# Fetching the context stream's mixing inputs ahead, and keeping its residual in DRAM

## The chip, the cores and the metric

The kernel runs on one core of one Trainium2 chip. The metric is the device time of one execution in microseconds, as the median of several runs. The core's engines are TensorE (PE; its weight loads are listed as PEld), VectorE (DVE), ScalarE (ACT), GpSimd (POOL) and SyncE (SP), which here only issues DMAs. TensorE's clock is granted by a throttle and is shown as a fraction of full speed.

## The reference

One step of a hybrid backbone with two layers, run for two streams that share the weights: 256 context tokens and 1024 latent tokens, all in float32, with 1024 model columns. Each layer computes:

```python
h   = rmsnorm(x, norm1_w) * (1 + sc1) + sh1
p   = h @ w_in                      # columns for three mixers
att = block_attention(q, k, v)      # latent queries see cached context keys and latent keys
lru = gelu(p_gate) * (hf + hb)      # bidirectional recurrence after a width-4 convolution
hy  = hyena_mixer(p_hy)             # width-3 convolution, two gated FFT convolutions
x   = x + g1 * (concat([att, lru, hy]) @ w_out)
h2  = rmsnorm(x, norm2_w) * (1 + sc2) + sh2
x   = x + g2 * ((silu(h2 @ ffn_w1) * (h2 @ ffn_w3)) @ ffn_w2)
```

The outputs are both streams' x after two layers, and the context's keys, values and final recurrence states of each layer.

## The kernel before

Activations lie with model columns on the partitions (eight tiles of 128) and tokens along the row. The latent stream has two blocks of 512 tokens, called l0 and l1; the context stream is one block of 256, called cc (`self.ctxs`, `cs`, and `s` where a function serves both). Float32 matmuls are made of three passes over a rounded high part and a remainder (`mm3`, L153 to L155); `split` makes the two parts, a ScalarE copy (L159) and a subtract (L160) that runs on VectorE unless another engine is named.

A planner puts the instructions of each engine in one order ahead of time, from a simulated timeline and from priorities; context mixing (`ctx_mix`) runs at a raised priority (`tc.high_priority(offset=3000)`) among the matmuls of latent Hyena and latent attention. Nearly all DMAs are issued from SP's queue, in that order. Memory in SBUF is given out in scoped pools: a pool that opens where an older one lay waits until the older one's last use, a store included, is over.

One layer runs so: the norm, w_in (its output goes to DRAM as pT, for both streams), the mixers of both streams (each stores its part of mix_l or mix_c to DRAM), w_out, the upper half of the feed-forward part (ffn_up) and its lower half (ffn_down). Of the context stream:

- `ctx_mix` opens a pool for each mixer in turn: cm (attention, L855 to L947), cl (LRU), ch (Hyena).
- `lru_pass` (from L1000) takes for each of two column tiles a gate weight gw (one buffer; GpSimd memset L1004), an input xp with padding (VectorE memsets L1010 and L1011, load L1012), and later a gate input gl (loaded by L1059); its result is stored at L1068 as mix_c<-xc.
- `conv` in Hyena (L1298 to L1306) takes for each of six tiles an input hxp with two padding columns (memsets L1301 and L1302, load L1303) from one pool tag, and the convolution writes hv (ScalarE, L952) and others. The matrices hw (L1320) and the spectra kt (L1234) are loaded there too.
- `w_out` (L453 to L490) loads the mixers' output for the blocks cc, l0, l1 in pieces of two tiles (tile mst for latent, mrow for context; load L467) and splits them into h (L469). The latent residual is loaded here from DRAM (xq<-xd_l, L473); the context residual stays in SBUF for the whole kernel, in the pool gp. `one` does the matmuls of one output tile, adds to the residual (L480) and stores a latent tile back (L482).
- `ffn_down` makes seven passes of eleven steps; the context takes part in passes 1 and 3. The latent residual is loaded in passes 0 and 1, a tile for each of steps 1 to 8 (x_l<-xd_l, L707); weights come as wst<-in_ffn_w_dram (L689) and are split into whl. At the end of layer 0 it also makes the next layer's norm (`nx`) and stores the latent residual again.
- `front0` loads both streams' x, the context's into gp, and stores the latent residual.

Of the kernel before, what the change touches and what calls it, by code (L numbers as in the profile page):

```python
# [87 lines left out]
class Net:  # L88
# [363 lines left out]

    def w_out(self, l, hp, tp, cp):  # L453
        nc = self.nc
        l0, l1, cc = self.all
        blks = (cc, l0, l1)
        for s, bi, b0, N in blks:
            self.h_new(s, bi, hp)
            mv = s.mix[l].rearrange("(k p) t -> p k t", p=128)
            for k0 in KPIECES:  # L460
                if s.lat and bi == 0 and k0 > 3:
                    st = self.wp.tile([128, 2, N], F32, tag="wst", name="mst", bufs=SBUFS)
                elif s.lat:
                    st = tp.tile([128, 2, N], F32, tag="gl", name="mst", bufs=3)
                else:
                    st = self.rows([128, 2, N])
                nc.sync.dma_start(st, mv[:, k0:k0 + 2, b0:b0 + N])  # L467
                h, k = s.h[bi][k0 // 4], k0 % 4
                self.split(st, h[:, 0, k:k + 2], h[:, 1, k:k + 2])  # L469
            if s.lat:  # L470
                s.x[bi] = [cp.tile([128, 4, 512], F32, tag=f"xq{bi}{j}", name=f"xq{bi}{j}") for j in range(2)]
                for d in range(0, 8, XD):
                    nc.sync.dma_start(s.x[bi][d // 4], s.xd[bi][:, d:d + XD])  # L473

        def one(m, w, s, bi, b0, N):
            ps = self.ps(s, "ops", (128, N))
            for i, k in enumerate(KORDER):
                self.mm3(ps, w[:, 0, k], w[:, 1, k], *self.hk(s, bi, k), i == 0, i == 7)
            xs = self.xs(s, bi, m)
            nc.vector.scalar_tensor_tensor(xs, ps, self.mod(l, s, 2, m), xs, ALU.mult, ALU.add)  # L480
            if s.lat:
                nc.sync.dma_start(s.xd[bi][:, m], xs)  # L482
            self.ss_add(s, tp, s.ss[bi], xs, m)

        for g in GROUPS:
            ws = [self.wtile(self.a["w_out"][l][:, m * 128:(m + 1) * 128].rearrange("(k p) m -> p k m", p=128))
                  for m in g]
            for b in blks:
                for m, w in zip(g, ws):
                    one(m, w, *b)  # L490
                if g[-1] == 7:
                    if b[0].lat:
                        self.norm_q(b[0], l, b[1], tp)
                    else:
                        self.norm(b[0], l, 1, b[1], hp, tp)
# [161 lines left out]
    def ffn_down(self, l, hp, pool, xp, last):  # L657
# [13 lines left out]
        def nx(s, bi):  # L671
            if last:
                self.store_y(s, bi, pool)
                return
            self.norm(s, l + 1, 0, bi, hp, pool)
            if s.lat:
                nc.sync.dma_start(s.xd[bi], s.x[bi])

        for n, (quads, op, q, outs, ctx, nxt) in enumerate(DOWN):
            wide = [self.ps(lat, "py") for _ in range(4)]  # L680
# [2 lines left out]
            for p in range(H):  # L683
                t = self.wp.tile([128, 2, 2, 512], F32R, tag="whl", name="whl", bufs=WBUFS)
                src = [a["ffn_w2"][l][(j * H + p) * 128:(j * H + p + 1) * 128, i * 512:(i + 1) * 512] for i, j in quads]
                A, B = t[:, 0], t[:, 1]
                st = self.wp.tile([128, 2, 512], F32, tag="wst", name="wst", bufs=SBUFS)
                for i in range(len(src)):
                    nc.sync.dma_start(st[:, i], src[i])  # L689
                if n:  # L690
                    gr = pool.tile([128, 2, 512], F32, tag="gl", name="gr", bufs=3)
                    br = gr[:, 0]
                else:
                    br = st[:, 1]
                nc.sync.dma_start(br, lat.gd[q, p])
                if ctx:
                    C = self.wp.tile([128, 2, 2, 512], F32R, tag="whl", name="whl", bufs=WBUFS)
                    for j in range(2):
                        self.split(st[:, j], C[:, j, 0], C[:, j, 1], nc.gpsimd)
                if len(src) == 2:  # L700
                    nc.vector.tensor_tensor(st[:, 0], st[:, 0], st[:, 1], op)  # L701
                self.split(st[:, 0], A[:, 0], A[:, 1], nc.gpsimd)
                self.split(br, B[:, 0], B[:, 1], nc.vector)
                if n < 2 and 0 < p < 9:
                    if p == 1:
                        self.x_new(lat, 1 - n, xp, 2)
                    nc.sync.dma_start(lat.x[1 - n][:, p - 1], lat.xd[1 - n][:, p - 1])  # L707
                for m in range(4):
                    c = slice(m * 128, (m + 1) * 128)
                    self.mm3(wide[m], A[:, 0, c], A[:, 1, c], B[:, 0], B[:, 1], p == 0, p == H - 1)  # L710
                if ctx:
                    g = pool.tile([128, 2, 512], F32R, tag="gk", name="gk", bufs=1)
                    nc.sync.dma_start(gr[:, 1, 0:256], cs.gd[p])
                    nc.sync.dma_start(gr[:, 1, 256:512], cs.gd[H + p])
                    self.split(gr[:, 1], g[:, 0], g[:, 1], nc.vector)
                    for j in range(2):
                        for k in range(2):
                            c = slice(256 * j + k * 128, 256 * j + (k + 1) * 128)
                            self.mm3(yc[k], g[:, 0, c], g[:, 1, c], C[:, j, 0], C[:, j, 1], j == p == 0,
                                     j == 1 and p == H - 1)  # L720
# [240 lines left out]
    def lru_consts(self):  # L961
# [21 lines left out]
        for l in range(DEPTH):  # L983
            gb = self.gp.tile([128, 8], F32, name=f"gb5_{l}")
            nc.vector.tensor_scalar(gb, self.col(l, "lru_gate_b", 0, 8), 0.5, None, ALU.mult)
            self.gb5.append(gb)

    def lru(self, s, l, pool):
        nc, a = self.nc, self.a
        T = s.T  # L990
        if s.lat:
            for ct in range(2):
                self.lru_pass(s, l, pool, (ct,))
        else:
            self.lru_pass(s, l, pool, (0, 1))

    def lru_pass(self, s, l, pool, cts):
# [2 lines left out]
        nd = 1 if s.lat else 4  # L1000
        tiles = []
        for ct in cts:
            gw = pool.tile([128, 2, 2, 128], F32, tag="gw", name="gw")
            nc.gpsimd.memset(gw, 0.0)  # L1004
            for b in range(2):
                nc.sync.dma_start(
                    gw[64 * b:64 * b + 64, :, :, 64 * b:64 * b + 64].rearrange("i d g j -> i (d g) j"),
                    a["lru_gate_w"][l, :, :, 2 * ct + b].rearrange("d g i j -> i (d g) j"))
            xp = pool.tile([128, T + 3], F32, tag=f"xp{ct % len(cts)}", name="xp", bufs=1)
            nc.vector.memset(xp[:, 0:2], 0.0)  # L1010
            nc.vector.memset(xp[:, T + 2:T + 3], 0.0)  # L1011
            nc.sync.dma_start(xp[:, 2:T + 2], s.pT[l][768 + ct * 128:896 + ct * 128, :])  # L1012
            xc = pool.tile([128, T], F32, tag=f"xc{ct % len(cts)}", name="xc", bufs=1)
            self.dwconv(xc, xp, [self.col(l, "lru_conv_w", 2 * k + ct) for k in range(4)], T,
                        self.col(l, "lru_conv_b", ct))
            tiles.append((gw, xp, xc))
# [38 lines left out]
                hs[ct].append(h)  # L1055
        for ct in cts:
            xp, xc = tiles[cts.index(ct)][1:]
            gl = pool.tile([128, T], F32, tag="la" if s.lat else f"gl{ct}", name="gl")
            nc.sync.dma_start(gl, s.pT[l][1024 + ct * 128:1152 + ct * 128, :])  # L1059
            t1, t2 = xp[:, 0:T], xc  # L1060
            nc.scalar.activation(t1, gl, AF.Square)
            nc.vector.tensor_scalar(t1, t1, 0.044715, 1.0, ALU.mult, ALU.add)
# [231 lines left out]
    def hy_conv(self, s, l, pool, xtag="hxp"):  # L1294
# [2 lines left out]

        def conv(j, ct, tag, op):  # L1298
            i = 2 * j + ct
            xp = pool.tile([128, T + 2], F32, tag=xtag, name="hxp")  # L1300
            nc.vector.memset(xp[:, 0:1], 0.0)  # L1301
            nc.vector.memset(xp[:, T + 1:T + 2], 0.0)  # L1302
            nc.sync.dma_start(xp[:, 1:T + 1], s.pT[l][1280 + i * 128:1408 + i * 128, :])  # L1303
            out = op.tile([128, T], F32, tag=tag, name=tag, bufs=2)
            self.dwconv(out, xp, [self.col(l, "hy_conv_w", 6 * k + i) for k in range(3)], T,
                        tmp=op.tile([128, T], F32, tag="y", name="ht", bufs=2) if tag == "hx" and s.lat else None)  # L1306
# [41 lines left out]
def hybrid_kernel(ctx: ExitStack, tc: tile.TileContext, a: dict):  # L1348
# [42 lines left out]
    def front0(hp):  # L1391
        net.sq = ("ft", FT)
        with scoped(net, "lt0", "left") as tp, scoped(net, "lx0", "left") as xp:
# [8 lines left out]
            net.mods_now(0, 3)  # L1402
            net.mods_add(0, 0, 16)
            net.load_x(lat, a["x_sample"], tp, None, 1)
            net.load_x(cs, a["x_prompt"], tp, gp, 0)
            net.norm(lat, 0, 0, 0, hp, tp)
            net.norm(lat, 0, 0, 1, hp, tp)
            net.norm(cs, 0, 0, 0, hp, tp)
            step(TAPS[0])
            for bi in range(2):  # L1410
                for d in range(0, 8, 4):
                    nc.sync.dma_start(lat.xd[bi][:, d:d + 4], lat.x[bi][d // 4] if bi else lat.x[bi][:, d:d + 4])
# [23 lines left out]
            net.hyena_pre(lat, l, hq, hvp, "hxp" if l else "kt")  # L1436

    def ctx_mix(l):
        with scoped(net, f"cm{l}", "right") as p:
            net.attention(cs, l, p, p)  # L1440
        with scoped(net, f"cl{l}", "right") as p:
            net.lru(cs, l, p)
        with scoped(net, f"ch{l}", "right") as p:
            net.hyena_pre(cs, l, p, p)
            net.hyena(cs, l, p, p, p)

    def lat_mix(l, lks):
        with scoped(net, f"ya{l}", "left") as pa:
# [138 lines left out]
```

## Time and profile before

| | |
|---|---|
| median of 3 runs | 3712.36 us (3709.19 to 3715.75) |
| the profiled execution's own time | 3711.6 us |
| its span on the core | 3709.8 us |
| mean granted TensorE clock | 0.971 |
| TensorE busy | 3497.4 us (94%) |
| VectorE busy | 2331.7 us (63%) |
| ScalarE busy | 1433.2 us (39%) |
| GpSimd busy | 1439.6 us (39%) |

The profile is of one execution. A matmul's end is modelled, so a busy TensorE is not one at its peak. A row of the timeline has its start, the busy time of one or several like instructions in a row (x38), engine, line, operation, output <- inputs, shapes, and in brackets how long the engine sat idle before it and what ended this. SPq is SP's queue; the time of its rows is that of issuing DMAs, not of the transfers. A row of windows has the window, its length, the busy time and count of PE, PEld, DVE, ACT and POOL, the granted clock, the busy share of the 16 DMA engines and the GB/s that they moved.

### The profile page before, as it was taken

What the parts mean: (1) busy time and instruction counts of PE and PEld (TensorE: products, weight loads), DVE (VectorE), ACT (ScalarE), POOL (GpSimd) and SP (SyncE); (2) the same over time, 40 slices, a digit from 0 to 9 for tenths busy, and PEclk for the clock granted to TensorE, in tenths of its full rate; (3) what the DMA queues carried; (4) which work ended last, traced back from release to release, by engine and by line L of the source; (5) the groups of instructions that cost most, each with busy time, mean ns of one, the idle gap of its engine ahead of it and who ended that gap; (6) DMA issues with size and microseconds to landing.
All of it is one profiled execution on the core that took longest, in us unless ns stands there. A gap on an engine that the chain in (4) does not pass through costs nothing.

```text
span 3709.8 us, 50289 instructions
## 1 busy us (share of the span) xinstructions
PE 3497.4 (94%) x18418; PEld 2785.8 (75%) x18418; DVE 2331.7 (63%) x4016; ACT 1433.2 (39%) x2347; POOL 1439.6 (39%) x940
## 2 busy tenths in 40 slices
PE   6989989999989999999999999999998999999997
PEld 3667776667768888887777787667686888887776
DVE  6554467877466565566685674777648565565655
ACT  4424344745342222224444543455424222223442
POOL 3332034110245555556654332200035555555652
PEclk7999999999999999999999999999998999999999
DMA  7565673310412222236674344520221222225665
GB/s 275 171 194 176 199 267 122 107 46 21 152 36 67 86 90 78 89 107 227 194 256 132 109 162 152 189 70 27 98 90 40 88 87 79 91 80 199 187 202 198
DMA packets 400893, 485.92 MB, mean 131 GB/s; under 512 B 38382, under 2 KB 250912, under 8 KB 397318
## 3 DMA queue, kind: packets, MB, share of 16 engines
q1 hardware_dynamic: 397510, 468.03, 38.5%
q0 software_dynamic: 3136, 14.68, 1.2%
q8 instruction: 145, 2.38, 0.3%
q14 instruction: 102, 0.84, 0.1%
HBM read 350.94 MB, written 131.67 MB: 130 GB/s over the span
## 4 chain that ended last, share of the span: by engine, by line
PE 60%; DVE 7%; DMA 7%; issue 4%; POOL 2%; ACT 2%; SPq 0%; DVEq 0%; ACTq 0%; POOLq 0%
PE pu L154 8%; PE pu L155 8%; PE pu L153 8%; PE pvo L938 4%; PE sps L903 4%; PE tps L919 3%; PE puv L153 2%; PE puv L154 2%; PE puv L155 2%; PE ops L155 2%; PE ops L154 2%; PE ops L153 2%; DMA wst<-in_ffn_w_dram 2%; POOL whl L160 2%; PE py L153 2%
## 5 line engine op out<-in xcount | busy, mean ns | idle before, releaser
L160 POOL TENSOR_TENSOR whl<-wst,whl 128x512 fp32r<-128x512 f32 (+1 forms) x463 | 894.0, 1940 | 864.0 <-ACT whl L159 842.7
L159 ACT ACTIVATE whl<-wst 128x512 fp32r<-128x512 f32 (+1 forms) x488 | 394.3, 825 | 853.5 <-PE pu L155 297.9
L153 PE MATMUL pu<-hq,whl 128*128 128x512 f32 x1232 | 490.0, 399 | 10.2 <-ACT hq L523 8.8
L155 PE MATMUL pu<-hq,whl 128*128 128x512 f32 x1232 | 488.9, 398 | 0.0
L153 PE MATMUL wps<-h,whl 128*128 128x512 f32 (+1 forms) x768 | 286.0, 374 | 4.7 <-ACT pe L440 2.2
L154 PE MATMUL pu<-hq,whl 128*128 128x512 f32 x704 | 281.4, 400 | 8.7 <-POOL hq L524 4.6
L154 PE MATMUL wps<-h,whl 128*128 128x512 f32 (+1 forms) x768 | 284.1, 370 | 1.9 <-POOL h L160 1.4
L155 PE MATMUL wps<-h,whl 128*128 128x512 f32 (+1 forms) x768 | 283.6, 370 | 0.0
L153 PEld LDWEIGHTS pu<-hq,whl 128*128 128x128 f32 x1232 | 234.2, 190 | 65.5 <-ACT hq L523 10.7
L155 PEld LDWEIGHTS pu<-hq,whl 128*128 128x128 f32 x1232 | 234.6, 190 | 55.1
L153 PE MATMUL py<-whl 128*128 128x512 f32 x616 | 224.2, 402 | 23.4 <-ACT whl L159 18.0
L154 PE MATMUL py<-whl 128*128 128x512 f32 x616 | 228.9, 396 | 0.2 <-DVE whl L160 0.2
L155 PE MATMUL py<-whl 128*128 128x512 f32 x616 | 221.0, 395 | 0.7 <-POOL whl L160 0.6
L154 PE MATMUL pu<-hl,whl 128*128 128x512 f32 x528 | 210.6, 399 | 8.8 <-POOL hl L524 8.8
L906 ACT ACTIVATE pq<-pq,mn 128x1280 f32<-128x1280 f32 (+1 forms) x160 | 190.2, 1190 | 70.1 <-DVE pq L904 65.4
L919 PE MATMUL tps<-ident,pq 128*128 128x128 f32 x1344 | 196.0, 277 | 17.6 <-DVE pk L921 9.0
L155 PE MATMUL puv<-h,whl 128*128 128x256 f32 x704 | 199.2, 283 | 5.2 <-POOL whl L160 5.2
L153 PE MATMUL puv<-h,whl 128*128 128x256 f32 x704 | 199.6, 283 | 0.3 <-ACT whl L159 0.3
L154 PE MATMUL puv<-h,whl 128*128 128x256 f32 x704 | 199.2, 283 | 0.0
L701 DVE TENSOR_TENSOR wst<-wst 128x512 f32<-128x512 f32 x110 | 133.8, 1219 | 102.3 <-POOL whl L160 68.9
L919 PEld LDWEIGHTS tps<-ident,pq 128*128 128x128 f32 x1344 | 156.4, 142 | 53.6 <-DVE pk L921 21.8
L904 DVE TENSOR_SCALAR_CACHE_REDUCE pq<-sps,mn 128x512 f32<-128x512 f32 (+1 forms) x256 | 155.8, 611 | 50.3 <-PE sps L903 46.0
(353 smaller groups left out, 8093.1 us busy)
## 6 DMA issues: line engine op xcount, KB each, us to landing
wst<-in_ffn_w_dram SPq DMA_DIRECT2D x264, 256.0 KB
wst<-in_ffn_w_dram SPq DMA_DIRECT2D x88, 512.0 KB
wst<-in_w_mod_dram SPq DMA_DIRECT2D x68, 512.0 KB
gr<-gd_l SPq DMA_DIRECT2D x132, 256.0 KB
gd_l<-gs SPq DMA_DIRECT2D x66, 256.0 KB
wst<-in_w_in_dram SPq DMA_DIRECT2D x32, 512.0 KB
wst<-in_w_mod_dram SPq DMA_DIRECT2D x14, 1024.0 KB
gd_l<-g SPq DMA_DIRECT2D x44, 256.0 KB
```

The source lines that it names most:

```text
L153: mm(ps, wh, xh, start=first, stop=False)
L154: mm(ps, wh, xl, start=False, stop=False)
L155: mm(ps, wl, xh, start=False, stop=last)
L159: nc.scalar.activation(hi, src, AF.Copy)
L160: (eng or nc.vector).tensor_tensor(lo, src, hi.bitcast(F32), ALU.subtract)
L701: nc.vector.tensor_tensor(st[:, 0], st[:, 0], st[:, 1], op)
L903: nc.tensor.matmul(p, qx[:, ts], kt[:, h, k0:k0 + kn], start=h == 0, stop=h == 1)
L904: nc.vector.tensor_scalar(pt[:, k0:k0 + kn], p, -1.0, mn[:, c - 1:c] if c else BIG, ALU.mult, ALU.min, accum_out=mn[:, c:c + 1])
L906: nc.scalar.activation(pt, pt, AF.Exp, bias=mn[:, len(chunks) - 1:], scale=-1.0, accum_out=ls[:, t:t + 1])
L919: nc.tensor.transpose(ps[:, k, t], pq[t][:, (t0 + k) * 128:(t0 + k + 1) * 128], self.ident)
L938: nc.tensor.matmul(ob[64 * hd:64 * hd + 64, 0], vx[:, t], pk[:, t].rearrange("p t q -> p (t q)"), start=t == nkt - 1, stop=t == 0)
```

## The change

A new pool ci is open around the context's three mixers. `ctx_in` takes from it, ahead of attention, a tile for each of the ten inputs that LRU and Hyena read (two xp, two gl, six hxp), sets the padding columns on GpSimd and issues the ten loads of 128 KB. LRU and Hyena of the context use these tiles in place of their own. `gate_w` holds what was the gate weight's code in `lru_pass`, with a buffer for each column tile of the context.

The context's residual no longer stays in SBUF. `front0` loads it into a pool of its own stage and stores it to DRAM (xd_c); `w_out` takes a tile and loads it behind the loads of the residual of l0, and stores each of eight tiles back as `one` has added to it; `ffn_down` takes a tile and loads it at pass 0, step 5; `nx` stores it after the norm of the next layer.

In `w_out`, the four context pieces of a layer are split by a GpSimd copy and a GpSimd subtract.

```diff
 def w_out(self, l, hp, tp, cp):
@@
-                self.split(st, h[:, 0, k:k + 2], h[:, 1, k:k + 2])
+                if s.lat:
+                    self.split(st, h[:, 0, k:k + 2], h[:, 1, k:k + 2])
+                else:
+                    nc.gpsimd.tensor_copy(h[:, 0, k:k + 2], st)
+                    nc.gpsimd.tensor_tensor(h[:, 1, k:k + 2], st, h[:, 0, k:k + 2].bitcast(F32), ALU.subtract)
@@
+            if bi == 0 and s.lat:
+                self.x_new(cs, 0, tp)
+                nc.sync.dma_start(cs.x[0], cs.xd[0])
@@
-            if s.lat:
-                nc.sync.dma_start(s.xd[bi][:, m], xs)
+            nc.sync.dma_start(s.xd[bi][:, m], xs)
@@ ffn_down, nx
-            if s.lat:
-                nc.sync.dma_start(s.xd[bi], s.x[bi])
+            nc.sync.dma_start(s.xd[bi], s.x[bi])
@@ ffn_down, steps
                 if n < 2 and 0 < p < 9:
+                    if n == 0 and p == 5:
+                        self.x_new(cs, 0, xp)
+                        nc.sync.dma_start(cs.x[0], cs.xd[0])
@@
+    def ctx_in(self, l, pool):
+        nc, a, s = self.nc, self.a, self.ctxs
+        T = s.T
+        s.pre = {}
+        for ct in range(2):
+            for nm, e0, e1, r0 in (("xp", 2, 1, 768), ("gl", 0, 0, 1024)):
+                t = s.pre[nm, ct] = pool.tile([128, e0 + T + e1], F32, tag=f"{nm}{ct}", name=nm)
+                if e0:
+                    nc.gpsimd.memset(t[:, 0:e0], 0.0)
+                    nc.gpsimd.memset(t[:, e0 + T:], 0.0)
+                nc.sync.dma_start(t[:, e0:e0 + T], s.pT[l][r0 + ct * 128:r0 + 128 + ct * 128, :])
+        for i in range(6):
+            t = s.pre["hx", i] = pool.tile([128, T + 2], F32, tag=f"hx{i}", name="hxp")
+            nc.gpsimd.memset(t[:, 0:1], 0.0)
+            nc.gpsimd.memset(t[:, T + 1:], 0.0)
+            nc.sync.dma_start(t[:, 1:T + 1], s.pT[l][1280 + i * 128:1408 + i * 128, :])
@@ lru_pass
-            gw = pool.tile([128, 2, 2, 128], F32, tag="gw", name="gw")
+            gw = self.gate_w(l, ct, pool, f"gw{ct % len(cts)}")
+            if s.lat:
...
+            else:
+                xp = s.pre["xp", ct]
@@ conv in Hyena
+            else:
+                xp = s.pre["hx", i]
@@ front0
-            net.load_x(cs, a["x_prompt"], tp, gp, 0)
+            net.load_x(cs, a["x_prompt"], tp, xp, 0)
@@
+            nc.sync.dma_start(cs.xd[0], cs.x[0])
@@ ctx_mix
+        with scoped(net, f"ci{l}", "right") as q:
+            net.ctx_in(l, q)
+            with scoped(net, f"cm{l}", "right") as p:
+                net.attention(cs, l, p, p)
+            with scoped(net, f"cl{l}", "right") as p:
+                net.lru(cs, l, p)
+            with scoped(net, f"ch{l}", "right") as p:
+                net.hyena_pre(cs, l, p, p)
+                net.hyena(cs, l, p, p, p)
```

## Rows read from the trace of the kernel before

**Rows 1.** The page of the kernel before: span and engines.

```profile
span 3709.8 us, 50289 instructions
...
PE 3497.4 (94%) x18418; PEld 2785.8 (75%) x18418; DVE 2331.7 (63%) x4016; ACT 1433.2 (39%) x2347; POOL 1439.6 (39%) x940
```

**Rows 2.** Windows of 10 us, LRU opening, layer 0; columns as explained above.

```profile
700.00:710.00 10.00, 10.00 (x72) 7.67 (x73) 9.08 (x30) 6.77 (x12) 0.53 (x1) 1.00 0.34 94
```

**Rows 3.** Windows of 10 us, Hyena opening of layer 0.

```profile
740.00:750.00 10.00, 7.32 (x46) 4.43 (x46) 7.59 (x20) 3.39 (x5) 1.75 (x2) 0.83 0.18 39
750.00:760.00 10.00, 5.70 (x38) 4.50 (x35) 2.83 (x9) 1.75 (x4) 1.06 (x3) 0.82 0.22 66
760.00:770.00 10.00, 10.00 (x54) 8.21 (x53) 9.48 (x35) 6.74 (x14) 1.40 (x3) 0.84 0.24 66
```

**Rows 4.** Timeline, Hyena opening, layer 0: start, us, engine, line, operation [idle before <-releaser].

```profile
745.22 6.22 PE L938 MATMUL pvo<-pk,vx0l 128*64 128x256 f32 x38
...
746.54 0.80 SPq L1068 DMA_DIRECT2D mix_c<-xc  x2
...
754.47 0.06 DVE L1301 MEMSET hxp<- 128x1 f32 x1 [6.88 <-DMA mix_c<-xc]
...
756.72 0.51 ACT L952 ACTIVATE hv<-hxp,cols 128x256 f32<-128x256 f32 x1 [9.47 <-DMA hxp<-pT_c]
...
758.41 1.97 PE L919 MATMUL tps<-ident,pq 128*128 128x128 f32 x8 [4.30 <-DVE pk L921]
```

**Rows 5.** Timeline of layer 1's context mixing, and one undisturbed run of matmuls.

```profile
2415.21 1.06 ACT L159 ACTIVATE h<-mst 128x1024 fp32r<-128x1024 f32 x1 [5.66 <-DMA mst<-mix_l]
...
2417.66 0.47 PE L919 MATMUL tps<-ident,pq 128*128 128x128 f32 x1 [5.84 <-ACT pq L906]
...
2418.06 6.51 PE L938 MATMUL pvo<-pk,vx0l 128*64 128x256 f32 x38
...
2425.52 0.52 ACT L952 ACTIVATE hv<-hxp,cols 128x256 f32<-128x256 f32 x1 [2.54 <-DMA hxp<-pT_c]
...
2651.28 4.53 PE L938 MATMUL pvo<-pk,vx1l 128*64 128x256 f32 x38
```

**Rows 6.** Windows of 10 us, start of context mixing, layers 0 and 1.

```profile
620.00:630.00 10.00, 10.00 (x74) 7.83 (x73) 4.78 (x11) 2.16 (x5) 3.82 (x4) 1.00 0.68 224
2250.00:2260.00 10.00, 8.80 (x64) 6.37 (x63) 5.51 (x7) 3.43 (x5) 6.59 (x6) 1.00 0.95 322
```

**Rows 7.** Window of 10 us, w_out of layer 0, during context pieces.

```profile
990.00:1000.00 10.00, 10.00 (x59) 8.70 (x58) 2.36 (x4) 2.45 (x4) 0.00 (x0) 1.00 0.27 85
```

**Rows 8.** Timeline, start of ffn_down, layers 0 and 1.

```profile
1673.52 3.69 SPq L707 DMA_DIRECT2D x_l<-xd_l  x8
...
1684.08 0.63 ACT L159 ACTIVATE whl<-wst 128x512 fp32r<-128x512 f32 x1 [7.21 <-DMA wst<-in_ffn_w_dram]
...
1685.76 1.20 PE L153 MATMUL py<-whl 128*128 128x512 f32 x4 [2.19 <-ACT whl L159]
...
3409.54 2.07 PE L153 MATMUL py<-whl 128*128 128x512 f32 x4 [3.21 <-ACT whl L159]
```

**Rows 9.** Windows of 10 us, start of ffn_down, layer 1.

```profile
3400.00:3410.00 10.00, 6.79 (x29) 5.35 (x29) 1.67 (x2) 1.66 (x3) 1.75 (x2) 0.93 0.98 335
3410.00:3420.00 10.00, 10.00 (x34) 7.86 (x34) 10.00 (x13) 4.20 (x8) 7.35 (x6) 0.73 1.00 360
```

**Rows 10.** Instructions of tile h, layer 0: count, ns minimum/median/maximum, first and last start.

```profile
L159 ACT ACTIVATE h<-mrow x4: 631/632/633, 985.8 to 999.0; 128x512 fp32r<-128x512 f32 x4
L160 DVE TENSOR_TENSOR h<-mrow,h x4: 681/692/694, 986.5 to 999.7; 128x512 fp32r<-128x512 f32 x4
L160 DVE TENSOR_TENSOR h<-mst,h x8: 1212/1223/3391, 671.6 to 980.5; 128x1024 fp32r<-128x1024 f32 x8
```

**Rows 11.** Page's group of a GpSimd operation: busy us, mean ns | idle before.

```profile
L652 POOL TENSOR_TENSOR gs<-g 128x512 f32<-128x512 f32 x66 | 86.3, 1308 | 88.0 <-DVE g L610 87.0 <-DMA gd_l<-gs 1.0
```

More of the change, by code (lines that the diff above doesn't have):

```diff
@@ L454, in w_out @@
         nc = self.nc
+        cs = self.ctxs
         l0, l1, cc = self.all
@@ L986, in lru_consts, with gate_w @@
             self.gb5.append(gb)
+    def ctx_in(self, l, pool):
[14 more added lines that the diff above has]
+            nc.sync.dma_start(t[:, 1:T + 1], s.pT[l][1280 + i * 128:1408 + i * 128, :])
+    def gate_w(self, l, ct, pool, tag):
+        nc, a = self.nc, self.a
+        gw = pool.tile([128, 2, 2, 128], F32, tag=tag, name="gw")
+        nc.gpsimd.memset(gw, 0.0)
+        for b in range(2):
+            nc.sync.dma_start(
+                gw[64 * b:64 * b + 64, :, :, 64 * b:64 * b + 64].rearrange("i d g j -> i (d g) j"),
+                a["lru_gate_w"][l, :, :, 2 * ct + b].rearrange("d g i j -> i (d g) j"))
+        return gw
     def lru(self, s, l, pool):
@@ L1002, in lru_pass @@
         for ct in cts:
-            gw = pool.tile([128, 2, 2, 128], F32, tag="gw", name="gw")
[L1004 to L1012, printed above, removed]
+            gw = self.gate_w(l, ct, pool, f"gw{ct % len(cts)}")
+            if s.lat:
+                xp = pool.tile([128, T + 3], F32, tag="xp0", name="xp", bufs=1)
+                nc.vector.memset(xp[:, 0:2], 0.0)
+                nc.vector.memset(xp[:, T + 2:T + 3], 0.0)
+                nc.sync.dma_start(xp[:, 2:T + 2], s.pT[l][768 + ct * 128:896 + ct * 128, :])
+            else:
+                xp = s.pre["xp", ct]
             xc = pool.tile([128, T], F32, tag=f"xc{ct % len(cts)}", name="xc", bufs=1)
@@ L1057, in lru_pass @@
             xp, xc = tiles[cts.index(ct)][1:]
-            gl = pool.tile([128, T], F32, tag="la" if s.lat else f"gl{ct}", name="gl")
-            nc.sync.dma_start(gl, s.pT[l][1024 + ct * 128:1152 + ct * 128, :])
+            if s.lat:
+                gl = pool.tile([128, T], F32, tag="la", name="gl")
+                nc.sync.dma_start(gl, s.pT[l][1024 + ct * 128:1152 + ct * 128, :])
+            else:
+                gl = s.pre["gl", ct]
             t1, t2 = xp[:, 0:T], xc
@@ L1299, in conv @@
             i = 2 * j + ct
[L1300 to L1303, printed above, removed]
+            if s.lat:
+                xp = pool.tile([128, T + 2], F32, tag=xtag, name="hxp")
+                nc.vector.memset(xp[:, 0:1], 0.0)
+                nc.vector.memset(xp[:, T + 1:T + 2], 0.0)
+                nc.sync.dma_start(xp[:, 1:T + 1], s.pT[l][1280 + i * 128:1408 + i * 128, :])
+            else:
+                xp = s.pre["hx", i]
             out = op.tile([128, T], F32, tag=tag, name=tag, bufs=2)
@@ L1438, in ctx_mix @@
     def ctx_mix(l):
[L1439 to L1445, printed above, removed]
+        with scoped(net, f"ci{l}", "right") as q:
[7 more added lines that the diff above has]
+                net.hyena(cs, l, p, p, p)
     def lat_mix(l, lks):
```

## The prediction

> **What bounds the kernel now.** I read the page first: TensorE is busy for 3497.4 of 3709.8 us, the other engines for 63% or less [rows 1]. So 3709.8 − 3497.4 = 212.4 us of TensorE idleness is all that a change of fetches, stores and side engines can win, apart from stretches at a lower granted clock. The changed code touches six places: the start of context mixing, the opening of its LRU and Hyena stages, w_out, ffn_down, and the two ends of a layer. So I next read ten-microsecond windows across those places, to see where TensorE is not at 10.00, and then the timeline there for what the engines wait for.
>
> The window views show little. The LRU opening is full: TensorE 10.00 at clock 1.00 [rows 2]. The Hyena opening of layer 0 is not: TensorE works 7.32 + 5.70 + 10.00 = 23.02 of 30 us at a granted clock of 0.82 to 0.84 [rows 3], so 6.98 us idle; 1.00 is 2.4 GHz, and a value between 0.5 and 1 is a mean over its two levels, 1.2 and 2.4 GHz. The timeline tells why [rows 4]. The LRU's result is stored at 746.54 (two DMAs); Hyena's pool lies in the memory that the LRU's pool gives back, and its first instruction, a VectorE memset of the input tile, starts at 754.47 with 6.88 us of idleness put down to that store. The input load is then issued, ScalarE's first use of the tile (hv, L952) starts at 756.72 with the load named as releaser, and TensorE, bound to its planned order, stands for 4.30 us until 758.41. Matmuls of latent attention in this stretch run at the lower clock: 38 of them take 6.22 us.
>
> Layer 1 has a similar stall of 5.84 us ending at 2417.66, but another cause [rows 5]: ScalarE sat 5.66 us behind mst<-mix_l, a load of the latent mix for w_out, and TensorE waits for ScalarE's pq. Context's hv comes only at 2425.52, with 2.54 us of waiting for its load, no TensorE row beside it. The same 38 matmuls take 6.51 us after this stall and 4.53 us at 2651.28, where nothing has stalled.
>
> **What the change does, part by part.**
>
> *Hyena and LRU inputs fetched ahead.* The six hxp, two xp and two gl loads leave the stage openings. What stays is the pool: hv's output is still the first tile of a pool that opens when the mix_c store has landed, and hw and kt are still loaded into it. So in layer 0 hv can start where the memset does now, at 754.47, and not before: 756.72 − 754.47 = 2.25 us [rows 4]. I take all of it off the 4.30 us stall: −2.25, with 2.05 us of stall left, and what is late next is the mix_c store itself. Its bounds: nothing, if hw and kt end last; at most the whole idleness and the whole clock loss of these 30 us, 6.98 + 23.02 × 0.17 = 10.9 us [rows 3]. In layer 1 hv's 2.54 us wait lies off TensorE's stall; I take half of it, −1.3, since an earlier context chain only shifts work. Bounds: nothing, and the stall with its clock dip, 5.84 + (6.51 − 4.53) = 7.8 us [rows 5]. The LRU opening gives nothing, since TensorE has no gap there [rows 2]; the separate buffer for each gate weight likewise.
>
> *The ten loads at the start of ctx_mix.* 10 × 131 KB = 1.31 MB for each layer, with ten issues on SP (some 4 us at the 0.4 us each that the store pair of [rows 4] takes) ahead of attention's own loads, and 16 short GpSimd memsets. At the traffic that now runs there, 224 and 322 GB/s [rows 6], these bytes are worth 5.9 and 4.1 us of DMA time. The bytes are not new, only early. TensorE is at 10.00 in layer 0 and at 8.80 in layer 1, DMA at 0.68 and 0.95, GpSimd at 3.82 and 6.59, so layer 0 has room and layer 1 less. I take +0.5 for each layer, +1.0; bounds nothing and 5.9 + 4.1 = 10.0, when all of it pushes a load that TensorE waits for.
>
> *Context residual in DRAM.* New traffic: in the opening one store of 1.05 MB; in each w_out a load of 1.05 MB and eight stores of 131 KB; in each ffn_down a load of 1.05 MB; after layer 0 a store. The first store is hidden by the layer's w_in matmuls that follow; nothing waits for it. The row stores of w_out leave while TensorE is at 10.00 and DMA at 0.27 [rows 7]: nothing, by the TensorE work of that stretch; if that cover were gone they would cost 1.05 / 0.335 = 3.1 us. The load in w_out goes in behind the latent loads, for a use in the last block: nothing, bound 3.1 each. The 8 KB a partition that the residual held are free, but no tile size follows it.
>
> The load in ffn_down is the one without cover. When its pool opens, SP issues eight x_l loads at once, taking 3.69 us [rows 8], and the weights stand behind them: ScalarE's split of a weight tile waits 7.21 us for wst and TensorE 2.19 us for that split; in layer 1 TensorE waits 3.21 us. DMA is at 0.98 to 1.00 and 335 to 360 GB/s [rows 9]. The new load (programmed at p = 5, among those eight) joins this burst. A saturated stretch that TensorE already waits on passes further bytes straight on: 1.05 MB / 0.335 = 3.1 us each, +6.2 in all. Bounds: nothing, if the weights are let past, and 3.1 + 10 × (1 − 0.73) = 5.8 us each where the stall also costs a window of clock such as the one after 3410 [rows 9], 11.6.
>
> *w_out's context splits.* Four pieces a layer move from a ScalarE copy (0.63) and a VectorE subtract (0.69, both [rows 10]) to a GpSimd copy and subtract. GpSimd's nearest row is an elementwise operation of the same shape, 1.31 us [rows 11]; so a piece takes at most 2 × 1.31 = 2.6 in place of 1.3, +1.3 each, +5.2 on GpSimd a layer. Neither end counts on TensorE now: it is at 10.00 where these pieces run and GpSimd at 0.00 [rows 7]. ScalarE and VectorE get 5.3 us back that nobody waits for, and the pieces come some microseconds later for matmuls of the last block. I take nothing; bounds nothing and 5.2 a layer.
>
> One VectorE row speaks against this step: subtracts of latent pieces take 1.22 us in the median but 3.39 at most [rows 10], beside weight splits on GpSimd. The Trainium skill, page "SBUF — State Buffer", section "Who interferes with whom", says that VectorE and GpSimd share a pair of ports under an exclusive lock, and that a VectorE instruction with two SBUF inputs contends with a GpSimd one that reads SBUF; both the moved subtracts and their neighbours are of that kind, and the long row agrees with it. Rival C is made from the long row alone.
>
> **The sum**, against the profiled execution's own 3711.6 us (span 3709.8; 0.8 below the median of the runs): −2.25 − 1.3 + 1.0 + 6.2 = +3.65, so 3715.3 us. A difference of 0.2%, 7.4 us, is about what this measurement can tell from none.
>
> **Rivals.**
>
> A, faster (0.25): the stalls go altogether. If the planned order moves hv and its chain past the openings, both layers win their upper bounds, 10.9 + 7.8 = 18.7, against costs of 7.2: 3711.6 − 18.7 + 7.2 = 3700.1. For it: layer 0's stall names the context chain, and each stall is followed by a low clock. Against: hv still writes into the pool that waits for mix_c, and layer 1's stall names mst<-mix_l.
>
> B, slower (0.17): the ten loads stand ahead of latent Hyena's and context attention's loads in SP's queue. It decides when one of those is needed within some 5 us of its issue. Then 10.0 takes the place of my 1.0: 3715.3 + 9.0 = 3724.3. For it: DMA 0.95 and TensorE 8.80 in layer 1 [rows 6]. Against: layer 0 has TensorE full.
>
> C, slower (0.04): GpSimd's splits hold up VectorE's subtracts and residual updates by 3.39 − 1.22 = 2.17 us [rows 10], twice a layer, on the path: 8.7, so 3724.0. Against: TensorE full at 990 to 1000.
>
> **How the numbers follow.** My forecast has 0.38, with a range of its own from 3707 to 3722 (ffn_down's load at nothing, or at its bound). The last 0.16 are for a planner that orders all instructions anew, by some 15 us either way. Faster by over 0.2%: A's most, 0.21, and 0.07 from the last case and my own lower end, 0.28. Slower: B's and C's 0.19, and 0.10 from the others, 0.29. Same: 0.43. The range is 3697 to 3729: A's and B's times with some 4 us beyond each.
>
> **What would show it.** Right: in layer 0's Hyena opening hv starts as the mix_c store lands, with no hxp load, and TensorE's stall is near 2 us; nine loads before the weights at ffn_down's start and a TensorE stall there longer by 3 us; TensorE full during w_out's context pieces. Wrong: the stalls of 4.30 and 5.84 us gone or grown (A, or a new order), TensorE idle within 10 us of ctx_mix's start (B), long VectorE rows beside GpSimd's splits (C), or no change at ffn_down's start.

## The result

The changed kernel takes 3745.98 us in the median of 5 runs (3737.71 to 3751.28), the kernel before 3712.36; the ratio is 1.0090, with a 95% interval of 1.0074 to 1.0105. So it is 34 us slower, where 3715.3 us and a range up to 3729 were forecast. The profiled execution has 3745.66 us, 34 above the 3711.6 of before.

The runs of the experiments stand on several chips, and each ratio is against runs of the kernel before beside them; there its median was 3711.35 us for the first four, 3715.95 for e6 to e9 and 3712.56 for e10 to e13. A ratio and the quotient of the medians differ by up to 0.14%, which is about what the times can tell.

Two lines of the page answer to [rows 1]: TensorE is busy 14.5 us longer, with as many matmuls, at a mean granted clock of 0.968 instead of 0.971, and idle for 3743.8 − 3511.9 = 231.9 us instead of 212.4.

```profile
span 3743.8 us, 50303 instructions
...
PE 3511.9 (94%) x18418; PEld 2791.5 (75%) x18418; DVE 2322.1 (62%) x3976; ACT 1426.4 (38%) x2339; POOL 1458.6 (39%) x988
```

To find where 34 us arise, one asks for the first and last start of a tile's matmuls in both traces. For w_in's wps in layer 0 (count, ns minimum/median/maximum, first and last start) before and after have:

```profile
L153 PE MATMUL wps<-h,whl x384: 274/392/803, 89.7 to 421.2; 128*128 128x512 f32 x129, 128*128 128x256 f32 x63
```

```profile
L153 PE MATMUL wps<-h,whl x384: 274/392/798, 92.6 to 431.7; 128*128 128x512 f32 x129, 128*128 128x256 f32 x63
```

w_in begins 2.9 us later and ends 10.5 us later. Context mixing begins with its first load: kt0c at 622.4 us before, the first of the ten loads at 640.8 after, 18.4 us later. The same question for other tiles gives the whole course (first start in us, the difference to before in brackets):

| stage | before | after |
|---|---|---|
| w_in, layer 0 (wps) | 89.7 | 92.6 (+2.9) |
| first load of context mixing, layer 0 | 622.4 | 640.8 (+18.4) |
| w_out, layer 0 (ops) | 938.2 | 959.0 (+20.8) |
| ffn_down, layer 0 (py) | 1656.2 | 1678.9 (+22.7) |
| w_in, layer 1 (wps) | 1958.1 | 1983.4 (+25.3) |
| w_out, layer 1 (ops) | 2672.0 | 2699.4 (+27.4) |
| ffn_down, layer 1 (py) | 3378.9 | 3406.8 (+27.9) |
| last py | 3699.2 | 3733.2 (+34.0) |

Over half of the loss is there before the first instruction of the fetches ahead. The two ffn_downs add 2.6 and 6.1 us; the other stages together add 6.9, of which the mixing of layer 0 has 2.4, w_in and mixing of layer 1 2.1, and w_out with ffn_up 1.9 and 0.5.

The three places that the forecast priced look so. Windows and timeline of the Hyena opening in layer 0, to be held against [rows 3] and [rows 4]:

```profile
760.00:770.00 10.00, 6.76 (x33) 4.48 (x33) 10.00 (x25) 2.65 (x4) 1.74 (x2) 0.83 0.13 29
770.00:780.00 10.00, 6.80 (x56) 4.62 (x51) 3.11 (x9) 3.90 (x8) 0.88 (x2) 1.00 0.22 50
780.00:790.00 10.00, 9.55 (x51) 7.62 (x52) 10.00 (x31) 4.85 (x9) 2.00 (x5) 0.83 0.17 55
```

```profile
766.49 1.22 PE L912 MATMUL sps<-kt0l,qx 128*128 128x512 f32 x2 [2.56 <-DVE pq L913]
...
768.66 0.80 SPq L1106 DMA_DIRECT2D mix_c<-xc  x2
...
777.13 0.33 SPq L1361 DMA_DIRECT2D hw<-in_c_hwc_dram  x1
...
777.17 0.91 ACT L961 ACTIVATE hv<-hxp,cols 128x256 f32<-128x256 f32 x2 [5.70 <-DMA mix_c<-xc]
...
779.12 0.47 POOL L1256 TENSOR_TENSOR pm<-hv 128x64 f32<-128x64 f32 x1 [12.28 <-DMA hw<-in_c_hwc_dram]
...
780.14 0.47 PE L1264 MATMUL xps<-ident,pm 128*128 128x128 f32 x1 [3.34 <-POOL pm L1257]
```

hv starts as the mix_c store lands, with no hxp load between, as forecast. But GpSimd's pm then waits for hw, loaded at 777.13, and TensorE for pm. That stall is 3.34 us, where 4.30 stood before and 2.05 were forecast. The 30 us hold 6.89 us of idleness, 6.98 before: the step was right and won nothing.

The start of context mixing in layer 0, against [rows 6], where TensorE stood at 10.00:

```profile
640.83 0.34 SPq L1008 DMA_DIRECT2D xp<-pT_c  x1
...
643.35 2.80 SPq L1013 DMA_DIRECT2D hxp<-pT_c  x6
646.20 0.43 SPq L864 DMA_DIRECT2D kt0c<-kd_c  x1
...
650.17 0.53 SPq L1272 DMA_DIRECT2D kt<-kf_l  x1
...
670.42 0.76 DVE L1286 TENSOR_TENSOR cm<-abps,kt 128x256 f32<-128x256 f32 x2 [7.29 <-DMA kt<-kf_l]
...
671.57 0.80 PE L912 MATMUL sps<-kt0c,qx 128*128 128x256 f32 x2 [3.37 <-DVE pq L913]
```

```profile
650.00:660.00 10.00, 7.98 (x35) 4.62 (x34) 5.93 (x17) 2.41 (x7) 1.47 (x2) 1.00 0.88 277
660.00:670.00 10.00, 8.21 (x44) 5.71 (x42) 3.14 (x9) 2.64 (x6) 1.48 (x2) 1.00 0.89 272
670.00:680.00 10.00, 8.43 (x27) 5.67 (x28) 4.06 (x15) 3.50 (x10) 1.97 (x3) 0.66 0.28 105
```

Ten loads leave first; latent Hyena's kt<-kf_l comes at 650.17 and later, VectorE waits 7.29 us for such a load, and TensorE loses 30 − 7.98 − 8.21 − 8.43 = 5.38 us, with the granted clock at 0.66 (a mean over 1.2 and 2.4 GHz) in the last ten.

The start of ffn_down in both layers, against [rows 8]:

```profile
1696.37 1.74 SPq L716 DMA_DIRECT2D x_l<-xd_l  x4
1698.16 0.43 SPq L713 DMA_DIRECT2D x_c<-xd_c  x1
1698.63 2.80 SPq L716 DMA_DIRECT2D x_l<-xd_l  x4
...
1710.64 2.07 PE L153 MATMUL py<-whl 128*128 128x512 f32 x4 [4.38 <-ACT whl L159]
...
3439.05 2.06 PE L153 MATMUL py<-whl 128*128 128x512 f32 x4 [4.91 <-ACT whl L159]
```

The new load stands among the first eight x_l loads, and TensorE's stalls behind the weights are 4.38 and 4.91 us, 2.19 and 3.21 before.

In w_out GpSimd's copy takes 0.61 us and its subtract 1.28 to 1.30 in both layers (one of 1.75), 1.9 a piece against the 2.6 that were the bound. The subtracts of latent pieces on VectorE are over when these pieces begin (last start 1001.1 against 1006.7 us in layer 0, 2719.8 against 2727.6 in layer 1). The longest of them are 2.17 and 3.40 us in the two layers, 3.39 and 3.40 before.

### The profile page after: what moved, and what is told of

It reads as the page before. It is cut to its first block, busy times and chain, and to the rows that moved or that the text cites. A ratio compares the mean times of both kernels' runs of the same rounds, so it can differ in the third digit from the quotient of the medians.

```text
span 3743.8 us, 50303 instructions
## 1 busy us (share of the span) xinstructions
PE 3511.9 (94%) x18418; PEld 2791.5 (75%) x18418; DVE 2322.1 (62%) x3976; ACT 1426.4 (38%) x2339; POOL 1458.6 (39%) x988
## 5 line engine op out<-in xcount | busy, mean ns | idle before, releaser
L707 DVE TENSOR_TENSOR wst<-wst 128x512 f32<-128x512 f32 x110 | 123.7, 1127 | 94.7 <-POOL whl L160 57.9
```

## The experiments

The theory held at first (R): the loss is the residual's, in the opening and in ffn_down. Its rivals: the ten loads (F), and any new order of the planner (A). The order can be read from two traces: write down the tiles of TensorE's matmuls one after the other and see where the lists part. The changed kernel's list leaves that of before at the 272nd matmul, in the opening, long before w_out or context mixing. There the kernel before goes on with the filter work (fp), the changed one with w_in (wps); before first, then after:

```profile
92.37 0.61 PE L385 MATMUL nps<-ident,nrr 128*128 128x128 f32 x4
92.81 1.02 PE L1120 MATMUL fp<-fw,h 65*128 65x512 f32 x2
```

```profile
95.44 0.61 PE L385 MATMUL nps<-ident,nrr 128*128 128x128 f32 x4
95.80 0.48 PE L153 MATMUL wps<-h,whl 128*128 128x512 f32 x1
```

**One part alone.** e1_fetch keeps the residual in SBUF; e2_resid has only the residual's move; e3_split only the GpSimd splits. e5_store adds one line to the kernel before:

```diff
@@ front0
             step(TAPS[0])
+            nc.sync.dma_start(cs.xd[0], cs.x[0])
```

e1_fetch: 

> Only the early fetch: the ten loads, the pool around the mixers and the buffers for the gate weight; the residual stays in SBUF, and w_out splits as before. Theory R (the loss is the residual's, and most of it arises before 700 us of layer 0): within 4 us of the kernel before, 3708 to 3716. Theory F (the loss is that of the ten loads, which stand ahead of latent loads in SP's queue): 15 to 22 us slower, 3727 to 3735. Theory A (any edit that makes the planner order anew loses): slower by 5 to 20 us.

e2_resid: 

> Only the residual in DRAM: the store in the opening, the load and eight stores in each w_out, the load in each ffn_down, the store after layer 0. Theory R: nearly the whole loss, 25 to 34 us slower, of it about 18 to 21 before 700 us and 3 in each ffn_down. Theory F: 6 us slower (ffn_down alone), 3718. Theory A: slower by 5 to 20 us.

e5_store: 

> The kernel before with one DMA more: the 1 MB store of the context residual in the opening, which nothing reads. By the planner's order of TensorE this kernel agrees with e2_resid up to layer 0's ffn_down. Theory R: slower by about 18 to 21 us, all before 700 us, no change after it. Theory F: within 3 us of before, since 1.05 MB at 335 GB/s are 3.1 us of DMA time. Theory A: slower by 5 to 20 us, anywhere.

e3_split: 

> Only the context splits of w_out on GpSimd; the planner's order differs from before's from layer 0's w_out on. Theories R and F: within 3 us of before, 3709 to 3715. Theory A: slower by 5 to 20 us, all after 950 us.

| run | median us | ratio to before | 95% interval |
|---|---|---|---|
| e1_fetch | 3840.83 | 1.0339 | 1.0319 to 1.0359 |
| e2_resid | 3735.26 | 1.0050 | 1.0033 to 1.0068 |
| e5_store | 3723.17 | 1.0026 | 1.0015 to 1.0036 |
| e3_split | 3717.55 | 1.0011 | 0.9997 to 1.0024 |

e2_resid and e5_store bear R out in kind, with smaller sizes than expected, and both also lie in theory A's 5 to 20 us: one store that nothing reads costs 0.26%, some 10 us. In e5_store context mixing starts at 643.4 us (kt0c), 21 later than before, and part of that is given back up to w_out (951.7, 13.5 later). e3_split is not told from no change. e1_fetch lies far outside what all three theories expected: 129 us slower. Its timeline shows why. The ten loads start at 625.86, but context attention's kt0c, which followed the opening of mixing at once before, is loaded at 927.91, 2 us after the last result store of latent attention (mix_l<-ot at 925.95):

```profile
625.86 0.56 SPq L1000 DMA_DIRECT2D xp<-pT_c  x1
...
927.91 0.33 SPq L856 DMA_DIRECT2D kt0c<-kd_c  x1
```

```profile
1000.00:1010.00 10.00, 0.00 (x0) 0.00 (x0) 5.49 (x8) 0.00 (x0) 3.26 (x3) 0.50 0.17 26
1010.00:1020.00 10.00, 0.77 (x2) 0.37 (x2) 3.28 (x10) 1.71 (x4) 0.96 (x2) 0.50 0.22 66
```

The context's mixers, no longer covered by latent matmuls, leave TensorE without work, its clock at 0.50 (1.2 GHz). The ten tiles take 10.3 KB of a partition (from their shapes); in the changed kernel the residual's 8 KB make room for them. That the pool of attention found no room beside them until latent attention gave its own back is argued from these sizes and times; no run shows it by itself.

**The store: bytes or order.** A store of half the residual leaves TensorE's order as before, in the trace to the last matmul. One of three quarters doesn't: it parts from before at the same matmul as e5_store, and from e5_store four matmuls on, so it is a third order and not e5_store's with fewer bytes.

```diff
-            nc.sync.dma_start(cs.xd[0], cs.x[0])
+            nc.sync.dma_start(cs.xd[0][:, 0:4], cs.x[0][:, 0:4])   # e6_half; 0:6 in e7_threequarters
```

e6_half: 

> The kernel before with a store of half the context residual (0.52 MB) in the opening, which nothing reads; TensorE's planned order is that of before, instruction by instruction. Theory O (the 1 MB store costs 12 us by the new order that the planner makes because of it): within 3 us of before. Theory T (it costs by its bytes and its place in the queue): half of e5_store's loss, 5 to 7 us slower.

e7_threequarters: 

> The same with three quarters of the residual (0.79 MB); here TensorE's planned order leaves that of before at the same instruction as in e5_store. Theory O: slower by 8 to 14 us, as e5_store, with the loss between 160 and 640 us. Theory T: three quarters of e5_store's loss, 8 to 10 us slower, and half of that in e6_half.

e6_half takes 3711.42 us, ratio 0.9995 (0.9983 to 1.0008); e7_threequarters 3718.88, 1.0017 (1.0006 to 1.0029). Half the bytes cost nothing, up to 3 us by the interval, where theory T wanted 5 to 7; with the new order the loss is there. The step between them speaks for O, but weakly: the 0.17% are 6 us, below the 8 to 14 that O expected, and the two intervals overlap a little. The traces say it more clearly. The last matmul of w_in in layer 0 starts between 420.9 and 424.5 us in the seven kernels whose order is that of before up to there (before, e1, e3, e6, e10, e12, e13) and between 427.8 and 434.1 in the seven with a new one, e7_threequarters the earliest of them. Nor does TensorE itself wait longer for transfers there: from 60 to 420 us its idleness put down to DMAs is 5.0 us before and 4.2 in e5_store. e10_late_store puts it to the test with all bytes, the changed kernel's whole remainder and the order of before up to context mixing:

```diff
-            net.load_x(cs, a["x_prompt"], tp, xp, 0)
+            net.load_x(cs, a["x_prompt"], tp, pf, 0)
-            nc.sync.dma_start(cs.xd[0], cs.x[0])
@@ fill, called by w_in
+        if l == 0 and i == 2:
+            tc.keep_in_program_order(nc.sync.dma_start(cs.xd[0], cs.x[0]))
```

e10_late_store: 

> The changed kernel, but the context residual lies in the pool of the filter work, and its full 1 MB store is issued at w_in's third column tile, behind everything programmed before it in SP's queue. TensorE's planned order then agrees with that of the kernel before up to context mixing. Theory O (the store's loss is one of the planned order): 9 to 13 us faster than the changed kernel, ratio to before 1.0055 to 1.0065, and w_in ends within 3 us of before's 421.4. Theory T (the bytes cost): as the changed kernel, 1.008 to 1.010, w_in's end at 430 or later.

e10_late_store takes 3719.82 us, ratio 1.0021 (1.0010 to 1.0031): 26 us are back, more than O expected. w_in runs from 90.0 to 423.0 us:

```profile
L153 PE MATMUL wps<-h,whl x384: 274/392/798, 90.0 to 423.0; 128*128 128x512 f32 x129, 128*128 128x256 f32 x63
```

The first of the ten loads leaves at 622.2, where the changed kernel has it at 640.8: 18.6 us of the difference are there when mixing begins, and w_out starts 2.4 us later than before instead of 20.8; the rest comes from layer 1's mixing on. O's 9 to 13 came from e5_store, whose mixing gives 7.5 of its 21 us back; in the changed kernel, with the ten loads in it, mixing gives nothing back. In e10_late_store the same block of loads costs TensorE nothing at first: it works 46.63 of the 50 us from 620, 46.36 before. One thing stays open: here the store is later and the order is that of before, and a full store at 62 us within the old order was never run. So order and place are told apart by e6_half alone, for half the bytes.

**The ten loads and ffn_down's load, in the changed kernel.** e8_after_att calls ctx_in behind context attention. e11_staggered does so too and ties its loads to attention's result stores:

```diff
+                with self.tc.issue_after(self.ots[0].ins):    # xp, gl; self.ots[2] for hxp
                     nc.sync.dma_start(t[:, e0:e0 + T], s.pT[l][r0 + ct * 128:r0 + 128 + ct * 128, :])
```

e9_down_late moves the load of the residual:

```diff
-                    if n == 0 and p == 5:
+                if n == 1 and p == 9:
                     self.x_new(cs, 0, xp)
                     nc.sync.dma_start(cs.x[0], cs.xd[0])
```

e8_after_att: 

> The changed kernel with the ten loads programmed behind context attention, so that in layer 0 attention's own loads (kt0c, vx0c, qx) stand ahead of them in SP's queue; nothing else is changed. Theory Q (the ten loads hold up attention's and latent Hyena's loads): 5 to 8 us faster than the changed kernel, 3738 to 3741, and TensorE idle for under 2 us between 640 and 680 instead of 5.4. Rival N (the loss in this stretch is one of order): 3743 to 3749.

e11_staggered: 

> The changed kernel with the ten loads kept apart: xp and gl are issued behind context attention's first result store, the six hxp behind its third. Theory Q (in one block the ten loads hold up latent Hyena's kt loads, and also in e8_after_att they still did): 5 to 9 us faster than the changed kernel, ratio 1.0065 to 1.0077, and TensorE idle under 1 us from 640 to 690 instead of 8. Rival N (order): 1.008 to 1.010, with other stalls in their place.

e9_down_late: 

> The changed kernel with the residual's load of ffn_down programmed in pass 1 at step 9 instead of pass 0 at step 5: in the queue it then stands behind all sixteen x_l loads and the first weights, not among the first eight. Theory D (the load stretches the first burst, and TensorE waits for the weights behind it): 4 to 7 us faster than the changed kernel, 3739 to 3742, with the stall at the first py matmul back near 2.2 and 3.2 us from 4.4 and 4.9. Rival M (the burst is as long wherever the bytes stand): 3743 to 3749.

e8_after_att takes 3741.84 us, ratio 1.0080 (1.0067 to 1.0093). TensorE's busy time from 640 to 690 us is 43.63, in the changed kernel 43.24: the stall in layer 0 stays, and its expected size was missed. e11_staggered takes 3737.52, 1.0064 (1.0051 to 1.0077), and the stall is gone. Windows of 50 us, first of the changed kernel, then of e8_after_att, of e11_staggered and of e2_resid, which has the changed kernel's order up to mixing and no early loads:

```profile
640.00:690.00 50.00, 43.24 (x198) 29.24 (x191) 25.82 (x80) 16.27 (x42) 8.05 (x27) 0.93 0.65 201
```

```profile
640.00:690.00 50.00, 43.63 (x213) 29.88 (x212) 28.25 (x87) 16.37 (x43) 9.55 (x28) 0.97 0.66 209
```

```profile
640.00:690.00 50.00, 49.65 (x250) 34.18 (x250) 35.63 (x102) 20.31 (x49) 8.70 (x28) 1.00 0.72 228
```

```profile
640.00:690.00 50.00, 49.51 (x245) 33.90 (x243) 37.11 (x112) 25.16 (x57) 11.81 (x13) 1.00 0.73 227
```

So in this order the block of ten loads holds up latent Hyena by 49.65 − 43.24 = 6.4 us of TensorE time, and kept apart they do not. It does so by standing ahead of the kt loads and not of attention's: VectorE waits for kt 18.2 us of these 50 in the changed kernel, 10.2 in e8_after_att and 6.7 in the other two. The interval of e11_staggered overlaps that of the changed kernel (from 1.0074) a little; the windows are what bears the verdict.

e9_down_late takes 3737.49 us, 1.0072 (1.0056 to 1.0088), 7 us below the changed kernel by the ratios, with overlapping intervals. In the traces the two ffn_downs, from the first py to the next layer's w_in or to the last py, take 301.3 and 322.5 us, 304.5 and 326.4 in the changed kernel, 301.9 and 320.3 before. The layer 1 figure is 323.9 to 326.8 in all five kernels with the early load and 316.9 to 322.9 in the nine others. The stalls at the first py matmuls are back at 1.28 and 2.15 us, as theory D has it:

```profile
1707.46 1.20 PE L153 MATMUL py<-whl 128*128 128x512 f32 x4 [1.28 <-ACT whl L159]
...
3429.54 1.21 PE L153 MATMUL py<-whl 128*128 128x512 f32 x4 [2.15 <-ACT whl L159]
```

**All repairs.** e12_all joins e10_late_store, e11_staggered and e9_down_late and puts the splits back; e13_all_split leaves them on GpSimd.

e12_all: 

> The changed kernel with four repairs: late store as in e10_late_store, loads kept apart as in e11_staggered, ffn_down's load late as in e9_down_late, context splits of w_out back on ScalarE and VectorE. If the terms add up (10, 7, 7 and up to 6 of 34 us): 3714 to 3722 where before is 3712, ratio 1.0005 to 1.0025. If the early loads then win what they were priced at: 0.999 to 1.0005. If the terms don't add up (each edit makes a new order): 1.004 or more.

e13_all_split: 

> As e12_all, with the context splits on GpSimd. Against e12_all this prices the splits. If they cost what e3_split's median shows: 3 to 6 us slower than e12_all. If that was nothing, as forecast: within 3 us of it.

e12_all takes 3715.88 us, ratio 1.0007 (0.9995 to 1.0018); e13_all_split 3717.86, 1.0017 (1.0008 to 1.0025). With the four repaired, the loss is gone within the interval, as expected for the sum. The terms don't add up singly: by the ratios the late store alone gives back 26 us, the loads kept apart 10 and ffn_down's load 7, some 42 where 33 were lost. The late store alone already takes the ten loads' stall away, so that stall is counted twice. Nothing is won either: no version here is told to be faster than the kernel before. The splits on GpSimd cost 0.10% by the difference, whose intervals overlap; the tiles of TensorE's matmuls stand in one order in both kernels.

## Why the prediction was wrong

The step that failed is a single sentence: "The first store is hidden by the layer's w_in matmuls that follow; nothing waits for it." Nothing waits for its data, and its bytes were rightly taken as cheap: half of them cost nothing at that place (e6_half), and with all of them at a later one mixing begins as early as before (e10_late_store). But with the store in the opening the planner orders TensorE's work anew from the 272nd matmul on. In that order w_in and latent Hyena's preparation lose 18.4 us up to the start of context mixing, and with the ten loads mixing starts with a stall that the other order doesn't have. e10_late_store, where the store leaves at 155.8 us instead of 62.1, has neither. A new order was counted among the cases, at 0.16 and "by some 15 us either way"; it should have been the first question for an edit that puts a transfer into the opening, and its size, with the stall that follows, was some 26 of the 34 us.

What in the new order loses isn't settled. Between w_in's end and the first load of mixing (201 us before, 209 after) TensorE's waits for X and pm, in latent Hyena's preparation, are longer; its two groups of the kernel before and of the changed one (busy us, mean ns | idle before, releasers):

```profile
L154 PE MATMUL abps<-X,hw 128*128 128x256 f32 x116 | 35.1, 304 | 1.1 <-DVE X L1229 1.1
...
L1226 PE MATMUL xps<-ident,pm 128*128 128x128 f32 x32 | 5.9, 294 | 2.6 <-POOL pm L1218 1.9 <-POOL pm L1219 0.5 <-DVE pm L1221 0.2
```

```profile
L154 PE MATMUL abps<-X,hw 128*128 128x256 f32 x128 | 38.4, 301 | 5.2 <-DVE X L1267 5.2
...
L1264 PE MATMUL xps<-ident,pm 128*128 128x128 f32 x32 | 6.9, 328 | 7.7 <-POOL pm L1256 3.5 <-POOL pm L1257 2.7 <-DVE pm L1258 1.2
```

They account for 5.2 − 1.1 + 7.7 − 2.6 = 9.2 us of such waits, and in e10_late_store, with the order of before, the two are back at 1.5 and 2.7. But the stretches don't hold the same work (128 abps matmuls against 116), and other waits are shorter: TensorE is idle 33.6 of 209 us against 29.5 of 201, so 4.1 us more in all. The granted clock is 0.92 against 0.94, and 10.5 of the 18.4 us had been lost by the end of w_in.

*Hyena inputs ahead, −2.25 and −1.3.* The mechanism is shown in layer 0, the gain isn't: the bound that was named, "nothing, if hw and kt end last", is what happened. In layer 1 the stall keeps the cause that the prediction read, the load of mst: ScalarE waits 5.13 us for it and TensorE 4.21 behind ScalarE, where it stood 5.84 in the kernel before, and a stall of 3.70 us stands ahead of it at 2426.45. Taking half of hv's wait off was wrong there; w_in and mixing of that layer together are 2.1 us longer.

```profile
2443.73 1.06 ACT L159 ACTIVATE h<-mst 128x1024 fp32r<-128x1024 f32 x1 [5.13 <-DMA mst<-mix_l]
...
2445.32 0.68 PE L928 MATMUL tps<-ident,pq 128*128 128x128 f32 x4 [4.21 <-ACT pk L932]
```

*Ten loads, +1.0.* Rival B's mechanism in layer 0: 5.38 us idle and a low clock, priced at 5.9. The forecast counted on a full TensorE there. In layer 1 there is no such stall, and the loads are no block there: they leave one after the other from 2199.4 to 2288.5 us, most of them long before attention's first load at 2288.9. The stall depends on the order too, since in e10_late_store the same block costs nothing in its first 50 us; why the new order makes it matter isn't shown.

*ffn_down, +6.2.* Right in place and mechanism. The two ffn_downs measure 2.6 + 6.1 = 8.7 us against before, within the bound of 11.6, and moving the load gives 3.2 + 3.9 = 7.1 of them back in the traces.

*w_out, nothing.* TensorE stays at 9.72 to 10.00 in the ten-microsecond windows of the context pieces, and rival C's collisions don't show: the latent subtracts are over by then, and in layer 0 VectorE's updates of the latent residual take 0.74 to 0.75 us each, as before. The Trainium skill, page "SBUF — State Buffer", section "Who interferes with whom", would let a VectorE instruction with two SBUF inputs wait for a GpSimd one that reads SBUF; no row here shows it for the context pieces. The 0.1% of e13_all_split against e12_all is not told from zero.

*SBUF.* "The 8 KB a partition that the residual held are free, but no tile size follows it" missed what e1_fetch points to: the fetch ahead seems to need that room, so that it can't be judged without the residual's move.

## What to carry to other kernels

Where a planner orders the instructions, a transfer that nobody waits for can cost more than its bytes: compare the two orders and see where they part before pricing a part at nothing; a smaller copy of the transfer that leaves the order alone, and a delayed one, help to tell order from bytes. Transfers fetched ahead in one block can push what stands behind them, so tie them to events of the stage before, and put a load that is needed late behind the burst that opens a stage. A tile that is kept longer can need room that another pool was using: look at when the next pool opens, not only at the loads.

## Not expected of the hardware

Little. The same kernel before ran from 3700.98 to 3724.49 us over the chips of these runs, 0.6%, more than the 0.2% that the forecast took as the measure's limit, so that steps under 4 us were settled by windows and starts in the traces, not by the times.
